# Scores, gate products and down projections issued in two halves around three products of the next weight unit

## The chip, the cores and the metric

The kernel runs on one core of one Trainium2 chip. The metric is the device time in microseconds (us); a run's time is that of its only core. Times of single executions come from the hardware profiler.

## What is computed

The reference is two transformer-like blocks on 256 tokens of width 1024, each with 16 meta tokens in front, all in float32. What matters here:

- Block one: a gated convolution mixer, then a layer of 16384 small experts. For each token and each of 8 heads a query of width 256 is scored against two sets of 128 sub-keys, `s1 = q[:128] @ keys1`, `s2 = q[128:] @ keys2`; the 16 best of each are paired, the 16 best pairs name experts, and a softmax gives their gates. The experts' output is `sum(gelu(u[e] . x) * gate[e] * v[e])`.
- Block two: two kinds of attention with gates, then a feed-forward part `(silu(h @ w_gate) * (h @ w_up)) @ w_down` with 2816 hidden columns.

The kernel does the expert layer densely: it computes `u . x` for all 16384 experts, multiplies by a gate that is zero nearly everywhere, and multiplies by `v`.

## The kernel before

**Units of weights.** All weights come as 453 units of 128 x 1024 floats. `load_to` (L124) starts the DMAs, five ahead. `split_to` (L145) splits each unit into a rounded half `hi` (ScalarE, L150) and the rest `lo` (VectorE, L152), two or three units ahead. `unit` (L155) hands out the next unit. A float32 product is then made of three rounded ones: hi x hi, hi x lo, lo x hi.

**Two ways to use a unit.** `mm_w` (L164) uses a unit as stationary weights: 8 slices of 128, three products each (L169 to L171), so 24 products with 256 moving columns into one PSUM bank. `mm_a` (L173) uses it as the moving side: two token halves, two column halves, three products each (L182 to L184), so 12 products with 512 columns into four banks that add up over many units.

**Plain float32 products.** Some small products are not split. They are single `matmul` calls with 128 columns on float32 data, and the trace has two records (passes) for each. The scores of a head (L539) are four such calls, so 8 passes; a gate group of four tokens (L675) is four calls, so 8 passes; there are 8 heads and 64 gate groups.

**The stages that the change touches.**

1. Route stage. The loop at L721 goes over 8 heads: two query units (`q`), then 7 expert units (`u`, `expert_in`, L694). After every unit `pull` (L709) lets VectorE's side work go on: a list `todo` of Python generators, each of which yields its estimated cost in us. `pull(us)` adds `us` to a credit, at most up to twice `us`, and runs the first generator of the list until the credit is spent; a `yield None` ends the pull at once. A head's `route` (L532) first yields None, then issues the scores on TensorE, copies them out (L540) and picks the best 16 (costs 9.3 in all). `decode` (L555) costs 19.1 and comes twice, after heads 3 and 7; `softmax` (L594) and `flip` (L609) follow the last route. A head's units bring 2 x 1.4 + 7 x 1.5 = 13.3 of credit.
2. Gate stage. When that list is empty, `gates` (L643) takes its place, 2.4 of credit for each `u` unit. Step g builds the two sides of group g on VectorE (`ga` L662, `gb` L666; before every eighth group also three one-hot instructions, L653 to L657), issues the four products of group g - 1 on TensorE (L675), and takes group g - 2 out of PSUM (L685, L687). So the passes of a group stand between two `u` units. What is left when the units run out is done in one go (L754), and only then do the `v` units begin.
3. Feed-forward. The loop at L1083 goes over 22 slices: `fg` and `fu` (24 products each, L1086, L1090), then the down projection `fd` of the slice two before (12 products, L1107). The last two `fd` units come together (L1109).

**What sets the order.** TensorE and the DMA queue of SyncE run in the order in which the Python program issues their instructions (`manual_schedule`, L272). VectorE and ScalarE are ordered by a scheduler. Every tile buffer is handed on by semaphores.

Of the kernel before, what the change touches and what calls it, by code (L numbers as in the profile page):

```python
# [1 line left out]

# [48 lines left out]
def two_blocks(ctx, tc, x, feats, vecs, w_in, w_out, w_q, keys, u, v, final_g, meta2, w_in2, lams, w_gate,  # L51
               w_br_sb, w_br_df, w_out2, w_fg, w_fu, w_fd, final_g2, gains, out):
    nc = tc.nc
# [107 lines left out]
        return ready[n]  # L161


    def mm_w(ps, a, cols):  # L164
        hi, lo = unit()
        ahi, alo = a
        for k in range(KC):
            ks = slice(k * P, (k + 1) * P)
            nc.tensor.matmul(ps, hi[:, ks], ahi[:, k, cols], start=(k == 0), stop=False)  # L169
            nc.tensor.matmul(ps, hi[:, ks], alo[:, k, cols], start=False, stop=False)  # L170
            nc.tensor.matmul(ps, lo[:, ks], ahi[:, k, cols], start=False, stop=(k == KC - 1))  # L171

    def mm_a(acc, parts, first, last):  # L173
        ws = [unit(1 if last else 2) for _ in parts]
        for t in range(2):
            ts = slice(t * P, (t + 1) * P)
            for n, ((ahi, alo), (hi, lo)) in enumerate(zip(parts, ws)):
                for b in range(2):
                    bs = slice(b * 512, (b + 1) * 512)
                    ps = acc[2 * t + b]  # L180
                    end = last and n == len(parts) - 1
                    nc.tensor.matmul(ps, ahi[:, ts], hi[:, bs], start=first and n == 0, stop=False)  # L182
                    nc.tensor.matmul(ps, ahi[:, ts], lo[:, bs], start=False, stop=False)  # L183
                    nc.tensor.matmul(ps, alo[:, ts], hi[:, bs], start=False, stop=end)  # L184

    def col(name, i):
        o = _OFF[name] + i
# [344 lines left out]
    def route(hd, qT, kt):  # L532
        yield None
        s = pr.tile([P, 2, 2, P], F32, tag="s", name=f"s{hd}", bufs=2)
        pss = mm_tile(f"sc{hd}")
        pv = pss.rearrange("p (t f n) -> p t f n", t=2, f=2)
        for t in range(2):
            for half in range(2):
                nc.tensor.matmul(pv[:, t, half, :], qT[half][:, t * P:(t + 1) * P], kt[:, half, :], start=True, stop=True)  # L539
        nc.scalar.activation(s, pv, AF.Copy)  # L540
        vv = pr.tile([P, 2, 2, TOPK], F32, tag="vv", name=f"vv{hd}", bufs=2)
        for t in range(2):
            for half in range(2):
                yield from top16(s[:, t, half, :], vv[:, t, half, :], iu_a[:, half, t, hd, :], 0.3)
        cand = pr.tile([P, 2, 88], F32, tag="cand", name=f"cand{hd}", bufs=2)
        nc.vector.tensor_tensor(cand[:, :, 0:16], vv[:, :, 0, 0:1].broadcast_to((P, 2, 16)), vv[:, :, 1, :], op=ALU.add)
        for a0, na, nb, o in ((1, 3, 8, 16), (4, 12, 4, 40)):
            nc.vector.tensor_tensor(cand[:, :, o:o + na * nb].rearrange("p t (a b) -> p t a b", a=na),
                                    vv[:, :, 0, a0:a0 + na].unsqueeze(3).broadcast_to((P, 2, na, nb)),
                                    vv[:, :, 1, :nb].unsqueeze(2).broadcast_to((P, 2, na, nb)), op=ALU.add)  # L550
        yield 0.7
        for t in range(2):
            yield from top16(cand[:, t, :], vals_a[:, t, hd, :], pos_a[:, t, hd, :], 0.26)
# [89 lines left out]
    def gates():  # L643
        pg, eT, gT, ah, al = (later[n] for n in ("pg", "eT", "gT", "ah", "al"))
        B32 = 32
        sides, banks = {}, {}
        for g in range(NG + 2):
            if g < NG:
                t0 = 4 * g
                if t0 % B32 == 0:  # L650
                    ts = slice(t0, t0 + B32)
                    o8 = pg.tile([P, B32, 8], F32, tag="o8", name=f"o8_{g}")
                    nc.vector.tensor_tensor(o8, ah[:, ts].unsqueeze(2).broadcast_to((P, B32, 8)),  # L653
                                            io128[:, :8].unsqueeze(1).broadcast_to((P, B32, 8)), op=ALU.is_equal)
                    nc.vector.tensor_tensor(o8, o8, gT[:, ts].unsqueeze(2).broadcast_to((P, B32, 8)), op=ALU.mult)
                    o16 = pg.tile([P, B32, TOPK], F32, tag="o16", name=f"o16_{g}")
                    nc.vector.tensor_tensor(o16, al[:, ts].unsqueeze(2).broadcast_to((P, B32, TOPK)),  # L657
                                            io16.unsqueeze(1).broadcast_to((P, B32, TOPK)), op=ALU.is_equal)
                    yield 1.6
                tl = slice(t0 % B32, t0 % B32 + 4)  # L660
                a = pg.tile([P, 4, P], F32, tag="ab", name=f"ga{g}", bufs=4)
                nc.vector.tensor_tensor(a.rearrange("p t (h l) -> p t h l", h=8),  # L662
                                        o8[:, tl, :].unsqueeze(3).broadcast_to((P, 4, 8, TOPK)),
                                        o16[:, tl, :].unsqueeze(2).broadcast_to((P, 4, 8, TOPK)), op=ALU.mult)
                b = pg.tile([P, 4, P], F32, tag="ab", name=f"gb{g}", bufs=4)
                nc.vector.tensor_tensor(b, eT[:, 1, t0:t0 + 4].unsqueeze(2).broadcast_to((P, 4, P)),  # L666
                                        io128.unsqueeze(1).broadcast_to((P, 4, P)), op=ALU.is_equal)
                sides[g] = (a, b)
                yield 1.4
            if 0 <= g - 1 < NG:  # L670
                a, b = sides.pop(g - 1)
                ps = at_tile(f"gp{g - 1}")
                p3 = ps.rearrange("p (c t) -> p c t", t=4)
                for i in range(4):
                    nc.tensor.matmul(p3[:, :, i], b[:, i, :], a[:, i, :], start=True, stop=True)  # L675
                banks[g - 1] = p3
            if g >= 2:
                j = g - 2
                p3 = banks.pop(j)
                n = seen[0]  # L680
                for tile_, c0, c1 in ((ew[0], 0, NA), (ew[1], NA, NK)):
                    m = min(max(n, c0), c1)
                    if m > c0:
                        o = tile_[:, j, :m - c0, :]
                        nc.vector.tensor_tensor(o, p3[:, c0:m, :], o, op=ALU.mult)  # L685
                    if m < c1:
                        nc.scalar.activation(tile_[:, j, m - c0:, :], p3[:, m:c1, :], AF.Copy)  # L687
                gated[0] = j + 1
                yield 0.2 + 0.55 * n / NK

    def chunk(c):
# [68 lines left out]
    def expert_w(i):  # L760
# [7 lines left out]
        wts[i] = hi2[:, 0, :], lo2[:, 0, :]  # L768
        wts[i + 1] = hi2[:, 1, :], lo2[:, 1, :]

    expert_w(0)
    while nu < NK:
        expert_in(nu)
# [309 lines left out]
    for m in range(NFF + 1):  # L1083
# [20 lines left out]
            nc.vector.tensor_tensor(lo, fa, hi.bitcast(F32), op=ALU.subtract)  # L1104
            prev.append((hi, lo))
        if 1 < m < NFF:
            mm_a(acc, [prev[m - 2]], m == 2, False)  # L1107
        elif m == NFF:
            mm_a(acc, prev[-2:], False, True)  # L1109
    table(AF.Sqrt)  # L1110
# [82 lines left out]
```

## Time and profile before

| what | value |
|---|---|
| median of 3 runs | 1479.19 us (1478.61 to 1486.41) |
| profiled execution, its own time | 1478.11 us |
| span of its instructions | 1476.4 us |
| mean granted TensorE clock | 0.997 |
| busy: TensorE products, weight loads, VectorE, ScalarE | 98%, 91%, 72%, 51% |
| route stage | about 125 to 377 us |
| gate stage with units, and its rest | 385 to 584 us, 584 to 597 us |
| feed-forward with down projections | about 1290 to 1469 us |

The span runs from the first to the last instruction; 1.7 us of the execution's own time lie around it. Starts of instructions are in us from the span's start, to 0.01 us. The end of a product is modelled, so the pace of TensorE is read from the starts: the start of one product to that of the next.

### The profile page before, as it was taken

How to read it: one execution, taken by the hardware profiler on the slowest of the kernel's cores; microseconds unless marked ns; L12 is line 12 of the kernel's file. 1: busy time of each engine (PE TensorE's matmuls, PEld its weight loads, DVE VectorE, ACT ScalarE, POOL GpSimd, SP SyncE). 2: the span in 40 equal slices, each digit the busy share in tenths (PEclk: the TensorE clock that was granted, in tenths of full speed). 3: DMA queues.
4: the chain of work that ended last, by engine and by line, in shares of the span. 5: the costliest groups of instructions: out<-in, count | busy, mean ns of one | idle time of the engine just before them, and what ended most of it. 6: DMA issues, size and time to landing. Idle time of an engine off the chain costs nothing.

```text
span 1476.4 us, 25739 instructions
## 1 busy us (share of the span) xinstructions
PE 1446.7 (98%) x10096; PEld 1338.5 (91%) x10096; DVE 1059.0 (72%) x1936; ACT 746.6 (51%) x1312; POOL 14.1 (1%) x32
## 2 busy tenths in 40 slices
PE   8999999999999999999999999999999999999998
PEld 7988999999999999788888888889998999899997
DVE  8987669779788999655555565755577776766665
ACT  7556444445444443344444445655455674554444
POOL 0010000000000000000000000100000000000000
PEclk9999999999999999999999999999999999999999
DMA  7626666665544444466666676633334456556662
GB/s 236 199 72 201 197 177 193 189 184 186 168 140 143 143 144 129 141 192 195 188 196 196 191 252 190 190 125 115 127 115 130 128 171 184 165 186 194 187 187 98
DMA packets 69816, 248.96 MB, mean 169 GB/s; under 512 B 7744, under 2 KB 9152, under 8 KB 69696
## 3 DMA queue, kind: packets, MB, share of 16 engines
q1 hardware_dynamic: 68544, 243.13, 52.9%
q0 software_dynamic: 1152, 4.19, 0.8%
q8 instruction: 79, 1.29, 0.4%
q14 instruction: 41, 0.34, 0.1%
HBM read 245.20 MB, written 2.10 MB: 168 GB/s over the span
## 4 chain that ended last, share of the span: by engine, by line
PE 93%; DVE 5%; issue 1%; DMA 0%; ACT 0%; SPq 0%; DVEq 0%; ACTq 0%
PE v L184 8%; PE v L182 8%; PE v L183 8%; PE u L171 7%; PE u L169 7%; PE u L170 7%; PE gp L675 4%; PE fg L170 1%; PE fu L171 1%; PE fg L171 1%; PE fu L170 1%; PE fd L184 1%; PE fu L169 1%; PE fg L169 1%; PE fd L183 1%; PE fd L182 1%
## 5 line engine op out<-in xcount | busy, mean ns | idle before, releaser
L152 DVE TENSOR_TENSOR lo<-raw,hi 128x1024 fp32r<-128x1024 f32 x453 | 552.9, 1223 | 241.4 <-ACT hi L150 239.9
L150 ACT ACTIVATE hi<-raw 128x1024 fp32r<-128x1024 f32 x453 | 478.6, 1058 | 469.7 <-PE u L170 122.7
L169 PE MATMUL u<-hThi,hi 128*128 128x256 f32 x1024 | 289.9, 283 | 0.0
L171 PE MATMUL u<-hThi,lo 128*128 128x256 f32 x1024 | 285.3, 279 | 0.1
L170 PE MATMUL u<-hTlo,hi 128*128 128x256 f32 x1024 | 284.9, 278 | 0.0
L182 PE MATMUL v<-hi,w_hi 128*128 128x512 f32 x512 | 199.3, 389 | 1.3 <-ACT w_hi L764 1.3
L184 PE MATMUL v<-hi,w_lo 128*128 128x512 f32 x512 | 199.3, 389 | 0.5 <-DVE w_lo L766 0.5
L183 PE MATMUL v<-lo,w_hi 128*128 128x512 f32 x512 | 199.2, 389 | 0.0
L170 PEld LDWEIGHTS u<-hTlo,hi 128*128 128x128 f32 x1024 | 194.0, 189 | 0.0
L171 PEld LDWEIGHTS u<-hThi,lo 128*128 128x128 f32 x1024 | 192.3, 188 | 0.8 <-DVE lo L152 0.7
L169 PEld LDWEIGHTS u<-hThi,hi 128*128 128x128 f32 x1024 | 192.5, 188 | 0.0
L182 PEld LDWEIGHTS v<-hi,w_hi 128*128 128x128 f32 x512 | 96.1, 188 | 21.4 <-ACT w_hi L764 1.5
L184 PEld LDWEIGHTS v<-hi,w_lo 128*128 128x128 f32 x512 | 96.1, 188 | 20.9 <-DVE w_lo L766 1.0
L183 PEld LDWEIGHTS v<-lo,w_hi 128*128 128x128 f32 x512 | 96.1, 188 | 20.1 <-DVE lo L152 0.2
L675 PE MATMUL gp<-ga,gb 128*128 128x128 f32 x512 | 66.6, 275 | 4.0 <-DVE gb L666 4.0
L764 ACT ACTIVATE w_hi<-ewa 128x512 fp32r<-128x512 f32 x48 | 30.2, 632 | 76.7 <-PE v L183 65.9
L675 PEld LDWEIGHTS gp<-ga,gb 128*128 128x128 f32 x512 | 61.7, 191 | 4.8 <-PE gp L675 3.6
L766 DVE TENSOR_TENSOR w_lo<-ewa,w_hi 128x512 fp32r<-128x512 f32 x48 | 33.2, 693 | 38.6 <-ACT w_hi L764 38.6
L662 DVE TENSOR_TENSOR ga<-o,o 128x512 f32<-128x512 f32 x64 | 44.0, 687 | 17.8 <-PE gp L675 17.3
L170 PE MATMUL fg<-hTlo,hi 128*128 128x256 f32 x176 | 49.2, 280 | 0.5 <-DVE hTlo L223 0.5
L169 PE MATMUL fg<-hThi,hi 128*128 128x256 f32 x176 | 49.3, 280 | 0.3 <-ACT hThi L222 0.3
L171 PE MATMUL fu<-hThi,lo 128*128 128x256 f32 x176 | 49.1, 279 | 0.0
(403 smaller groups left out, 2970.6 us busy)
## 6 DMA issues: line engine op xcount, KB each, us to landing
raw<-in_u_dram SPq DMA_DIRECT2D x128, 512.0 KB, 3.6
raw<-in_v_dram SPq DMA_DIRECT2D x128, 512.0 KB, 3.6
raw<-in_w_in_dram SPq DMA_DIRECT2D x67, 512.0 KB, 3.6
raw<-in_w_fg_dram SPq DMA_DIRECT2D x22, 512.0 KB, 3.6
raw<-in_w_fu_dram SPq DMA_DIRECT2D x22, 512.0 KB, 3.6
raw<-in_w_fd_dram SPq DMA_DIRECT2D x22, 512.0 KB, 3.6
raw<-in_w_out_dram SPq DMA_DIRECT2D x16, 512.0 KB, 3.6
raw<-in_w_q_dram SPq DMA_DIRECT2D x16, 512.0 KB, 4.3
```

The source lines that it names most:

```text
L150: latest["hi"] = nc.scalar.activation(hi, loaded[i], AF.Copy)
L152: latest["lo"] = nc.vector.tensor_tensor(lo, loaded[i], hi.bitcast(F32), op=ALU.subtract)
L169: nc.tensor.matmul(ps, hi[:, ks], ahi[:, k, cols], start=(k == 0), stop=False)
L170: nc.tensor.matmul(ps, hi[:, ks], alo[:, k, cols], start=False, stop=False)
L171: nc.tensor.matmul(ps, lo[:, ks], ahi[:, k, cols], start=False, stop=(k == KC - 1))
L182: nc.tensor.matmul(ps, ahi[:, ts], hi[:, bs], start=first and n == 0, stop=False)
L183: nc.tensor.matmul(ps, ahi[:, ts], lo[:, bs], start=False, stop=False)
L184: nc.tensor.matmul(ps, alo[:, ts], hi[:, bs], start=False, stop=end)
L662: nc.vector.tensor_tensor(a.rearrange("p t (h l) -> p t h l", h=8), o8[:, tl, :].unsqueeze(3).broadcast_to((P, 4, 8, TOPK)), o16[:, tl, :] ...
L675: nc.tensor.matmul(p3[:, :, i], b[:, i, :], a[:, i, :], start=True, stop=True)
L764: nc.scalar.activation(hi, a, AF.Copy)
L766: nc.vector.tensor_tensor(lo, a, hi.bitcast(F32), op=ALU.subtract)
```

## The change

Products can now be put off: `pend` is a list of pieces of work, and `flush(n)` issues the first n of them. `mm_w` issues the first half of what is pending before its first slice and the rest after the three products of its first slice. Scores, gate products and the down projections of the feed-forward part go through this list, each as two halves: two calls (4 passes) for scores and gates, one token half (6 products) for a down projection. `route` yields None a second time between the scores and their copy. `gates` and `mm_a` issue what is still pending before they go on. The down projections in the `v` stage, in the attention's output and the last two of the feed-forward part stay as they were.

```diff
+    pend = []
+
+    def flush(n=None):
+        for f in pend[:n]:
+            f()
+        del pend[:n]
+
     def mm_w(ps, a, cols):
         hi, lo = unit()
         ahi, alo = a
+        flush((len(pend) + 1) // 2)
         for k in range(KC):
+            if k == 1:
+                flush()
             ks = slice(k * P, (k + 1) * P)
...
-    def mm_a(acc, parts, first, last):
+    def mm_a(acc, parts, first, last, late=False):
         ws = [unit(1 if last else 2) for _ in parts]
-        for t in range(2):
+
+        def tokens(t):
             ts = slice(t * P, (t + 1) * P)
...
+        if late:
+            pend.extend(partial(tokens, t) for t in range(2))
+        else:
+            flush()
+            tokens(0)
+            tokens(1)
...
-        for t in range(2):
+
+        def scores(t):
             for half in range(2):
                 nc.tensor.matmul(pv[:, t, half, :], qT[half][:, t * P:(t + 1) * P], kt[:, half, :], start=True, stop=True)
+
+        pend.extend(partial(scores, t) for t in range(2))
+        yield None
+        flush()
         nc.scalar.activation(s, pv, AF.Copy)
...
         for g in range(NG + 2):
+            flush()
             if g < NG:
...
-                for i in range(4):
-                    nc.tensor.matmul(p3[:, :, i], b[:, i, :], a[:, i, :], start=True, stop=True)
+
+                def pair(i0, a=a, b=b, p3=p3):
+                    for i in (i0, i0 + 1):
+                        nc.tensor.matmul(p3[:, :, i], b[:, i, :], a[:, i, :], start=True, stop=True)
+
                 banks[g - 1] = p3
-            if g >= 2:
+                fresh = [partial(pair, 0), partial(pair, 2)]
+            else:
+                fresh = []
+            if g < 2:
+                pend.extend(fresh)
+            else:
...
                 gated[0] = j + 1
+                pend.extend(fresh)
                 yield 0.2 + 0.55 * n / NK
...
-            mm_a(acc, [prev[m - 2]], m == 2, False)
+            mm_a(acc, [prev[m - 2]], m == 2, False, late=True)
```

## Rows read from the trace of the kernel before

**Rows 1.** The page: busy times, and the chain that ended last, by engine.
```profile
PE 1446.7 (98%) x10096; PEld 1338.5 (91%) x10096; DVE 1059.0 (72%) x1936; ACT 746.6 (51%) x1312; POOL 14.1 (1%) x32
...
PE 93%; DVE 5%; issue 1%; DMA 0%; ACT 0%; SPq 0%; DVEq 0%; ACTq 0%
```

**Rows 2.** Windows: length, busy us (instructions) by engine, granted clock, DMA share, GB/s.
```profile
124.50:376.60 252.10, 251.89 (x2179) 250.93 (x2178) 197.14 (x558) 127.75 (x191) 0.00 (x0) 1.00 0.61 188
385.40:583.70 198.30, 198.30 (x1731) 198.30 (x1730) 180.56 (x330) 87.75 (x235) 0.00 (x0) 1.00 0.46 142
583.70:596.60 12.90, 7.61 (x58) 6.61 (x56) 12.80 (x29) 2.02 (x5) 0.00 (x0) 1.00 0.13 45
```

**Rows 3.** Timeline of TensorE, the scores of heads 0 to 7: start us, us, instruction.
```profile
135.72 1.05 PE L539 MATMUL sc<-kt,qT 128*128 128x128 f32 x8
...
162.06 1.06 PE L539 MATMUL sc<-kt,qT 128*128 128x128 f32 x8
...
187.45 1.05 PE L539 MATMUL sc<-kt,qT 128*128 128x128 f32 x8
...
213.78 1.06 PE L539 MATMUL sc<-kt,qT 128*128 128x128 f32 x8
...
267.28 1.05 PE L539 MATMUL sc<-kt,qT 128*128 128x128 f32 x8
...
285.13 1.06 PE L539 MATMUL sc<-kt,qT 128*128 128x128 f32 x8
...
302.37 1.05 PE L539 MATMUL sc<-kt,qT 128*128 128x128 f32 x8
...
323.05 1.06 PE L539 MATMUL sc<-kt,qT 128*128 128x128 f32 x8
```

**Rows 4.** Timeline of TensorE, three gate groups and second products behind two of them.
```profile
480.00 1.05 PE L675 MATMUL gp<-ga,gb 128*128 128x128 f32 x8
...
483.72 1.06 PE L675 MATMUL gp<-ga,gb 128*128 128x128 f32 x8
...
484.74 0.28 PE L170 MATMUL u<-hTlo,hi 128*128 128x256 f32 x1
...
487.36 1.05 PE L675 MATMUL gp<-ga,gb 128*128 128x128 f32 x8
...
488.37 0.28 PE L170 MATMUL u<-hTlo,hi 128*128 128x256 f32 x1
```

**Rows 5.** Timeline of TensorE, first product of down projections 0, 1 and 2.
```profile
1301.94 0.39 PE L182 MATMUL fd<-hi,f_hi 128*128 128x512 f32 x1
...
1310.20 0.39 PE L182 MATMUL fd<-hi,f_hi 128*128 128x512 f32 x1
...
1318.65 0.39 PE L182 MATMUL fd<-hi,f_hi 128*128 128x512 f32 x1
```

**Rows 6.** Timeline of TensorE, two gate groups of the rest.
```profile
588.61 1.13 PE L675 MATMUL gp<-ga,gb 128*128 128x128 f32 x8 [0.73 <-DVE gb L666]
590.48 1.13 PE L675 MATMUL gp<-ga,gb 128*128 128x128 f32 x8 [0.74 <-DVE gb L666]
```

**Rows 7.** Timeline of VectorE, start of a one-hot block, and what follows.
```profile
544.01 0.41 DVE L653 TENSOR_TENSOR o<-eT,io 128x256 f32<-128x256 f32 x1
544.34 0.68 DVE L657 TENSOR_TENSOR o<-al,io 128x512 f32<-128x512 f32 x1
544.94 1.22 DVE L152 TENSOR_TENSOR lo<-raw,hi 128x1024 fp32r<-128x1024 f32 x1
```

**Rows 8.** Timeline of TensorE, a group of four passes amid 256-column products.
```profile
1290.19 0.60 PE L231 MATMUL rsf_b<-rsf_d,ones 128*128 128x128 f32 x4
...
1290.75 0.28 PE L170 MATMUL fg<-hTlo,hi 128*128 128x256 f32 x1
```

**Rows 9.** Waits between 120 and 600 us: who for whom: us, times, longest us.
```profile
DVE ga L662 <- PE gp L675: 17.3, 32, 1.3
...
PEld u L171 <- DVE lo L152: 0.7, 3, 0.3
```

More of the change, by code (lines that the diff above doesn't have):

```diff
@@ L1 @@
 from contextlib import ExitStack
+from functools import partial
 import concourse.bass as bass
@@ L769, in expert_w @@
         wts[i + 1] = hi2[:, 1, :], lo2[:, 1, :]
+    assert not pend
     expert_w(0)
```

## Prediction, made before the changed kernel had run

> **What bounds the kernel now.** I read the page first: TensorE is busy for 98% of the span and makes 93% of the chain that ended last [rows 1], so only its pace and its holes count. The windows by stage come next: in the route stage and the gate stage TensorE has next to no hole, at full granted clock; VectorE is busy for 180.6 of 198.3 us (91%) in the gate stage. Between 583.7 and 596.6 us it is the other way round: VectorE is busy for 12.8 of 12.9 us and TensorE for 7.6 [rows 2]. That is the rest of the gate work, when no unit is left.
>
> The pace inside a full stage has to be read from starts, in the timeline. From one of the first four scores to the next lie 9 units, 216 products, each time the same work. They take 26.34 us, then 25.39, then 26.33 [rows 3]. The difference of 0.95 us is 4.4 ns a product. The reader is to see that it alternates with the scores: 8 passes go by and the pace is the other one. Six units from 267.28 us take 17.85, the next six 17.24 [rows 3]. The gate stage does the same per unit: 3.72 us from group to group, then 3.64 [rows 4]; and so does the feed-forward part per pair of units, 8.26 us between down projections, then 8.45 [rows 5]. The 95 products from 1290.75 to 1301.94 us take 117.8 ns each [rows 5, 8]: that is the slow pace, and the fast one is then 113.4. So TensorE keeps one of two paces for as long as 256-column products follow each other, and a whole group of scores, gates or a down projection turns the pace over.
>
> **What the change adds and removes.** No product, DMA or VectorE instruction comes or goes; what changes is the order on TensorE, and the planner's bookkeeping.
>
> *The halves.* I expect a half to turn the pace over as a whole does. From fast, the first half leaves slow; three products on, the second half enters slow and leaves fast. So the route stage, fast up to its first scores, stays fast. Slow now are the units behind the first, third, fifth and seventh scores, 9 + 9 + 6 + 7 = 31 [rows 3]. 24 products x 4.4 ns is 0.106 us a unit: **-3.3 us**. In the gate stage every second unit is slow, 26 to 27 of the 53 that will follow a group: **-2.8 us**.
>
> The feed-forward part begins slow [rows 8], so its first half group would leave fast. But three products are few, and I take the pace not to have settled by the second half, which then enters as if slow too and leaves fast. Then all gaps are 8.26 us, and 9 of the 19 are 8.45 now: 9 x 0.19 = **-1.7 us**. If slow were carried through instead, the 10 fast gaps would become slow: +1.9. No row shows an entry after three products; these are the ends, and I take the first because a settled slow entry left fast each time.
>
> *The price of splitting.* From the start of a gate group to the second product behind it 1.01 to 1.02 us go by [rows 4], for 8 passes and one product. For 4 passes the one row is at 1290 us: 0.56 [rows 8]. Two halves with three products are then 0.56 + 2 x 0.118 + 0.56 = 1.36 us up to the second product after; the whole group and three products more are 1.02 + 3 x 0.113 = 1.36. So it is free to the rounding of the rows, 0.01 a time; settling after each half may cost as much again. I take 0.02 for 53 gate groups and 8 scores, whose passes are alike, and 0.01 for 19 down projections: **+1.4 us**; the ends are 0 and twice that.
>
> *The second None.* This moves the plan, and it costs. The copy of the scores comes one unit later, and the pull is broken off there, so that credit above the cap is lost. In heads 0 to 3 that costs nothing later, because the queue runs dry before the next head anyway (9.3 of work against 13.3 of credit). From then on decode's 19.1 keep the queue full. I followed the credit unit by unit: before, the queue is empty after unit 73, and the units end with 7 gate groups to do, which is what the trace has (56 weight loads in the rest [rows 2]). After, it is empty after unit 77, and 11 groups remain. Each of the rest takes 1.87 us, since TensorE waits for `gb` [rows 6], against 0.9 in the stage (1.02 less one product of 0.12 [rows 4]). The one-hot block of group 56 falls into the rest as well: 0.33 + 0.60 us from start to start, and 0.33 for its third, which has the size of the first: 1.26 [rows 7]. 4 x 1.87 + 1.26 - 4 x 0.9 = **+5.1 us**. Bounds: 3.9 (the block hides) and 6.5 (one group more and some arrears).
>
> *Waits.* The second half of a gate group ends three products later, 0.35 us, and `ga` two groups on waits for it: VectorE waits there 32 times now, 17.3 us in all [rows 9]. Behind it on VectorE stand the `lo` of coming units and `gb`. It would wait 0.35 longer once and then run with that lag; the sides are needed a unit later (3.6 us [rows 4]), so this hides. Without that slack it would show as gaps before gate products, at most 0.35 us x 53. In the feed-forward part ScalarE's split into the buffer of the `fd` unit is let go 0.35 us later too, and is used two units on, over 5 us: 0. SyncE's DMAs are issued by `unit` in the same order as before, and none waits for another thing: 0. POOL's queue is not passed. TensorE's weight loads wait for `lo` 0.7 us in all [rows 9], in the route stage; with the side work moved that may go or double: -0.7 to +0.7.
>
> **The sum**: -3.3 - 2.8 - 1.7 + 1.4 + 5.1 = -1.3 us. Against the profiled execution's own 1478.1 that is 1476.8. The median of the three runs lies 1.1 higher; I put the forecast in between, at **1477.2 us**.
>
> **A rule that speaks against it.** The rows show two paces for one and the same product, 117.8 and 113.4 ns [rows 3, 5, 8]. The Trainium skill, page "TensorE: Matmul & The Clock Gate", section "Back-to-back issue gap", gives one gap per width at full clock, N/2.4 + 2.5 ns, so 109 ns for 256 columns, whatever came before; by it the order of issue would be worth nothing, and the sum would hold the price and the rest alone. The rows disagree with it: two paces, both longer than the rule's.
>
> **Rivals.**
> 1. *The down projections carry the slow pace.* As forecast, but +1.9 for -1.7: 1480.4. For it: the part begins slow [rows 8], and two turns bring back what was. Against it: only that three products are few. Chance 0.20.
> 2. *Two halves count as one group* and turn the pace over once, so it goes on alternating. Price and rest are left: 1478.1 + 1.4 + 5.1 = 1484.6. For it: three products are few. Against it: nothing but that each group turned it so far. The skill's one-gap rule comes out here as well. Chance 0.15.
> 3. *Slower: a half group always leaves TensorE slow.* It decides at the first scores, 135.72 us. For it: the one group of four passes amid such products comes from slow and is followed by slow [rows 8]. Against it: it has other operands, and whole groups from slow left fast. Now fast would become slow: in the route stage 53 units (2115 products besides the scores [rows 2] are 88 units, less 31 and the 4 before the first scores), in the gate stage 27, so 80 x 0.106 = 8.5, and 10 x 0.19 = 1.9 in the feed-forward part; with 1.4 and 5.1 that is +16.9: 1495.0. Chance 0.12.
> 4. *The rest does not grow*, because VectorE makes up for the later start: -3.3 - 2.8 - 1.7 + 1.4 = -6.4, 1471.7. Against it: 91% busy [rows 2]. Chance 0.05.
>
> The forecast has 0.45; 0.03 is for what I don't see.
>
> **The numbers.** 0.5% (7.4 us) is about what a measurement of this kernel can tell from no change. Forecast and rivals 1 and 2 lie within it, rival 3 above, rival 4 at its lower edge. Faster 0.05, same 0.81, slower 0.14. The range takes in rivals 1 and 2, and below the forecast the bounds of the price (-1.4), of the rest (-1.2) and of the waits (-0.7): 1473.0 to 1486.0.
>
> **What would show it.** Right: scores with nine units between them near 25.4 us apart every time; gate groups 3.64 us apart every time; 88 passes in the rest, which lasts 21.6 us where it lasted 12.9; down projections 8.26 us apart throughout. Wrong: distances that still alternate (rival 2) or all have the upper value (rival 3), 8.45 us between down projections (rival 1), 56 passes in the rest (rival 4).

## The result and the profile after

The changed kernel's median is 1491.47 us (8 runs, 1481.71 to 1497.02) against 1480.12 for the kernel before (8 runs, 1478.61 to 1486.41): the ratio is 1.0064, with a 95% interval of 1.0046 to 1.0082. Timed again later it was 1488.57 (12 runs, 1481.29 to 1493.20), ratio 1.0051 (1.0034 to 1.0068). The forecast was 1477.2, the range 1473.0 to 1486.0: too low, and the sign is the wrong one. The 20 times also lie far apart: 8 between 1481.3 and 1485.8, 12 between 1487.9 and 1497.0.

The profiled execution took 1484.49 us (span 1482.8), 6.4 more than that of before. Its page, busy times and chain, answers to [rows 1]:

```profile
PE 1450.1 (98%) x10096; PEld 1342.4 (91%) x10096; DVE 1059.7 (71%) x1936; ACT 746.6 (50%) x1300; POOL 14.1 (1%) x32
...
PE 95%; DVE 3%; DMA 1%; issue 0%; ACT 0%; SPq 0%; POOL 0%; DVEq 0%; ACTq 0%
```

No work came or went, TensorE is as full as before, so the time is in its pace and in the order. First the scores, in the timeline of TensorE (start, length, instruction; first halves of heads 0 to 3):

```profile
136.20 0.60 PE L560 MATMUL sc<-kt,qT 128*128 128x128 f32 x4
...
161.61 0.60 PE L560 MATMUL sc<-kt,qT 128*128 128x128 f32 x4
...
187.01 0.60 PE L560 MATMUL sc<-kt,qT 128*128 128x128 f32 x4
...
212.42 0.60 PE L560 MATMUL sc<-kt,qT 128*128 128x128 f32 x4
```

They are 25.41, 25.40 and 25.41 us apart, where before 26.34 and 25.39 took turns [rows 3]. The reader sees the mechanism of the forecast at work: two halves give the pace back. But the stage did not stay fast. Further on in the same timeline, products of one unit:

```profile
232.50 0.28 PE L182 MATMUL u<-hTlo,hi 128*128 128x256 f32 x1
232.61 0.38 PE L183 MATMUL u<-hThi,lo 128*128 128x256 f32 x1
232.82 0.29 PE L181 MATMUL u<-hThi,hi 128*128 128x256 f32 x1
...
234.60 0.28 PE L181 MATMUL u<-hThi,hi 128*128 128x256 f32 x1
...
235.66 0.28 PE L181 MATMUL u<-hThi,hi 128*128 128x256 f32 x1
```

and in the timeline of VectorE what the product of 232.61 needs, its `lo`:

```profile
230.19 1.22 DVE L614 TENSOR_TENSOR oh<-oh,ifl 128x1024 f32<-128x1024 f32 x1
231.32 1.22 DVE L153 TENSOR_TENSOR lo<-raw,hi 128x1024 fp32r<-128x1024 f32 x1
```

The `lo` stood behind a multiply of `decode` and ends at 232.54. The product that reads it takes 0.21 us to the next start, 0.10 more than its neighbours. Before it the pace is 113.3 ns; from 234.60 to 235.66 lie 9 products, 117.8 ns each. This slow pace goes through the last four scores unchanged to the end of the stage (a second gap, of 163 ns at 252.50 us, left it slow): 1293 slow products, 879 fast ones (counted by the distance of starts; before 807 and 1270).

The gate stage, gate groups in the timeline of TensorE:

```profile
405.91 0.60 PE L703 MATMUL gp<-ga,gb 128*128 128x128 f32 x4
406.71 0.60 PE L703 MATMUL gp<-ga,gb 128*128 128x128 f32 x4
409.62 1.06 PE L703 MATMUL gp<-ga,gb 128*128 128x128 f32 x8
413.26 1.05 PE L703 MATMUL gp<-ga,gb 128*128 128x128 f32 x8
416.98 1.06 PE L703 MATMUL gp<-ga,gb 128*128 128x128 f32 x8
```

One group is split, the next three are whole, and the distances still go 3.64, 3.72. In the whole stage the trace has 29 lines of 8 passes, 7 of 12 and 27 of 4, so 17 groups are split and 36 not. 636 of 1081 products are slow (622 of 1196 before). Gate stage and rest in the windows (columns as in [rows 2]):

```profile
397.57:581.45 183.88, 183.88 (x1602) 183.88 (x1601) 167.30 (x307) 81.15 (x215) 0.00 (x0) 1.00 0.45 142
581.45:603.22 21.77, 13.50 (x92) 12.09 (x90) 21.42 (x48) 2.08 (x5) 0.00 (x0) 0.92 0.08 25
```

The rest lasts 21.77 us (12.9 to 13.1 before [rows 2]) and holds 88 passes (56 before). VectorE's wait for a gate bank in the list of waits is no longer than before [rows 9]:

```profile
DVE ga L688 <- PE gp L703: 15.3, 29, 1.3
```

The down projections, first products in the timeline of TensorE, answer to [rows 5]:

```profile
1309.88 0.39 PE L195 MATMUL fd<-hi,f_hi 128*128 128x512 f32 x1
...
1318.15 0.39 PE L195 MATMUL fd<-hi,f_hi 128*128 128x512 f32 x1
...
1326.41 0.39 PE L195 MATMUL fd<-hi,f_hi 128*128 128x512 f32 x1
```

8.27 and 8.26 us apart: fast throughout, in this execution.

### The profile page after: what moved, and what is told of

It reads as the page before. It is cut to its first block, busy times and chain, and to the rows that moved or that the text cites. A ratio compares the mean times of both kernels' runs of the same rounds, so it can differ in the third digit from the quotient of the medians.

```text
span 1482.8 us, 25725 instructions
## 1 busy us (share of the span) xinstructions
PE 1450.1 (98%) x10096; PEld 1342.4 (91%) x10096; DVE 1059.7 (71%) x1936; ACT 746.6 (50%) x1300; POOL 14.1 (1%) x32
## 4 chain that ended last, share of the span: by engine, by line
PE 95%; DVE 3%; DMA 1%; issue 0%; ACT 0%; SPq 0%; POOL 0%; DVEq 0%; ACTq 0%
PE u L181 8%; PE u L183 8%; PE u L182 8%; PE v L196 7%; PE v L197 7%; PE v L195 7%; PE gp L703 3%; PE fg L182 1%; PE fd L197 1%; PE fd L196 1%; PE fg L183 1%; PE fd L195 1%; PE fg L181 1%; PE fu L183 1%; PE fu L182 1%; PE fu L181 1%
## 5 line engine op out<-in xcount | busy, mean ns | idle before, releaser
L195 PEld LDWEIGHTS v<-hi,w_hi 128*128 128x128 f32 x512 | 96.1, 188 | 21.6 <-ACT w_hi L799 1.5
L703 PE MATMUL gp<-ga,gb 128*128 128x128 f32 x512 | 70.9, 280 | 7.0 <-DVE gb L692 7.0
L183 PE MATMUL fg<-hThi,lo 128*128 128x256 f32 x176 | 48.8, 277 | 0.0
```

## The experiments

Two questions were open: what the parts of the change cost one by one, and why the times lie so far apart. The table gives the profiled execution of each kernel, in us: its own time, the route stage from the first `q` product to the first transpose of `flip`, its slow products, the gate stage, the rest, and the feed-forward part from the first product of the first down projection to the last product of the nineteenth.

| kernel | time | route | slow in it | gate | rest | feed-forward |
|---|---|---|---|---|---|---|
| before | 1478.11 | 252.1 | 807 | 198.1 | 13.05 | 152.92 |
| changed | 1484.49 | 263.7 | 1293 | 183.9 | 21.78 | 151.71 |
| e1 one None | 1476.41 | 250.6 | 130 | 198.2 | 13.05 | 151.71 |
| e2 None only | 1483.65 | 264.1 | 1439 | 183.5 | 21.78 | 152.92 |
| e3 down only | 1480.60 | 253.2 | 922 | 198.1 | 13.05 | 151.71 |
| e4 scores only | 1476.82 | 250.6 | 86 | 198.1 | 13.05 | 152.92 |
| e5 gates split | 1477.34 | 249.0 | 205 | 196.6 | 13.05 | 155.08 |
| e6 transposes | 1479.99 | 250.3 | 206 | 200.6 | 13.06 | 151.71 |
| e10 first scores whole | 1486.25 | 255.9 | 2014 | 198.2 | 13.05 | 155.08 |
| repeat 1 (changed) | 1482.35 | 259.8 | 94 | 183.9 | 21.77 | 155.08 |
| repeat 2 (changed) | 1484.13 | 263.7 | 1178 | 183.9 | 22.03 | 151.71 |
| again (changed) | 1485.22 | 259.9 | 209 | 183.9 | 21.78 | 155.08 |
| e11 light decode | 1481.50 | 259.0 | 37 | 183.9 | 21.77 | 151.71 |
| repeat 3 (changed) | 1482.74 | 259.9 | 94 | 183.9 | 21.78 | 155.08 |
| repeat 4 (changed) | 1486.10 | 261.4 | 92 | 183.9 | 21.78 | 155.08 |
| repeat 5 (changed) | 1485.55 | 260.9 | 41 | 183.5 | 22.03 | 151.71 |
| e12 first whole, two None | 1490.67 | 268.2 | 2066 | 183.9 | 22.03 | 151.71 |
| repeat 6 (changed) | 1490.00 | 269.0 | 2141 | 183.9 | 22.03 | 151.71 |

With the second None the route holds four units more, 96 products or 10.9 us at the fast pace, so 252.1 before stands against 263.0 there. In the kernels with halves for the down projections the last column holds three products of the next unit more, 0.34 us at the fast pace. From the first product of the first down projection to the start of the last product of the last one, the same work in every kernel, it is 166.78 us before, and 165.23 (fast) or 168.78 (slow) in the changed kernel.

**e1: the change with one None, so with the plan of before.**

```diff
     def route(hd, qT, kt):
-        yield None
```

> The changed kernel with the first None of route taken out, so that a route has one None as before. Theory A (two halves give the pace back, so TensorE keeps whatever pace the last disturbance left, for hundreds of us; the plan's later start costs 5.1 us by itself): the rest of the gate work is back at 7 groups and about 12.9 us, the time is some 5 us below the changed kernel's, and single runs still scatter over 5 to 12 us, since a wait in the route stage still decides the pace of all that follows. Theory B (only the plan costs): the time is that of the kernel before within 1 us, and runs scatter no more than its own do, about 3 us.

Measured: 1477.93 us (10 runs), 0.9986 of before (0.9972 to 1.0). The halves by themselves cost nothing; the median is 2.5 us lower, and the interval reaches from no gain to 4.1 us.

**e2: the second None alone, everything else as before.**

```diff
+        yield None
         nc.scalar.activation(s, pv, AF.Copy)
```

> The kernel before with a second None between the scores and their copy, all groups issued whole. Theories A and B both: 11 groups in the rest, 21.6 us, +5.1 us (1483 to 1485). Theory A besides: distances between scores still alternate between the two paces, and the runs scatter as little as those of the kernel before. If instead the time stays within 1.5 us of before, the longer rest is paid back elsewhere and the plan is not a cost.

Measured: 1485.90 us (6 runs, 1483.65 to 1488.69), 1.0047 (1.0032 to 1.0061), +5.4 against the 1480.46 of before. The rest has its 88 passes and 21.78 us here too. The plan alone makes the kernel slower, by about what the forecast gave it.

**e3: halves for the down projections alone.** `late=True` in the feed-forward part; scores and gates as before.

> The kernel before with the down projections of the feed-forward part alone in two halves. Theory A: within a run all 19 distances between first products of down projections are equal, 8.26 us if the part begins fast and 8.45 us if it begins slow; time -1.7 or +1.9 us against before, and which one can differ from run to run. Theory C (a second half three products on always leaves fast, as forecast): all at 8.26 us whatever the part begins with, -1.7 us.

Measured: 1480.45 us (10 runs), 1.0006 (0.9992 to 1.002). The profiled part is 1.2 us shorter in the table's window, 1.55 over the same work; the whole kernel is not measurably faster.

**e4: halves for the scores alone**, with one None.

> The kernel before with the scores alone in two halves, one None. Theory A: from the first to the fourth scores nine units take 25.4 us each time; behind that the pace is the one that the waits for lo left (between about 225 and 255 us), and it stays until the transposes of flip near 377 us, also across the scores of heads 4 to 7; time between -3.3 us (all fast) and +4 us (slow from 235 us on). Forecast as it stood: all distances fast, -3.3 us.

Measured: 1477.92 us (10 runs), 0.9987 (0.9972 to 1.0003). The window of its route stage, the stretch at its start, and the list of waits in the stage:

```profile
124.90:375.50 250.60, 250.39 (x2179) 249.51 (x2178) 196.98 (x557) 128.65 (x191) 0.00 (x0) 0.99 0.61 189
...
121.90:128.70 6.80, 5.75 (x27) 5.27 (x27) 5.31 (x8) 3.77 (x6) 0.00 (x0) 0.50 0.09 34
```

```profile
PEld u L183 <- DVE lo L153: 1.0, 4, 0.3
```

Here the scores did what the forecast wanted: 86 slow products for 807. By 4.4 ns each that is 3.2 us; the stage is 1.5 shorter. The difference is not in the waits: 1.0 us of waits for `lo` stand here, and as many before, 0.7 for `u` [rows 9] and in the same list

```profile
PEld q L171 <- DVE lo L152: 0.3, 1, 0.3
```

It is in the second window: this route starts at half clock. Its first scores come 10.04 us after its first product; in e5 and e10, with the same products ahead of them and full clock, it is 8.47 us. Without these 1.6 us the stage would be 3.1 us shorter than before. e5, which starts at full clock, has that directly (249.0); e1 starts at half clock as e4 does.

**Repeats 1 and 2: the changed kernel, unedited.** Repeats 1 to 6 are single profiled executions of it.

> The changed kernel once more, unedited, for a second profile. Theory A (the pace is carried): same order of instructions, but another pace can be held in the route stage behind the waits for lo, and in the feed-forward part from its first units on; whatever the time differs from 1484.5 us is found as 4.4 ns a product (slow less fast) in these two stages, up to 4 us in the feed-forward part. Theory B (something else scatters): the paces are as in the first profile and the difference lies elsewhere.

> The same as the look before, a third profile of the changed kernel: Theory A: times of 1490 us and more show the slow pace in both stages, times near 1482 the fast pace in at least one. Theory B: no such relation.

Repeat 1 has a fast route and a slow feed-forward part, repeat 2 the reverse. Of repeat 1 the route's window, its waits for `lo`, and its down projections:

```profile
124.80:384.60 259.80, 259.59 (x2275) 258.67 (x2273) 201.77 (x562) 133.94 (x199) 0.00 (x0) 1.00 0.61 190
```

```profile
PEld u L183 <- DVE lo L153: 0.7, 3, 0.3
```

```profile
1304.19 0.39 PE L195 MATMUL fd<-hi,f_hi 128*128 128x512 f32 x1
...
1312.64 0.39 PE L195 MATMUL fd<-hi,f_hi 128*128 128x512 f32 x1
...
1321.09 0.39 PE L195 MATMUL fd<-hi,f_hi 128*128 128x512 f32 x1
```

8.45 us apart, both times, where the execution above has 8.27. The same instructions, the other pace, and it is kept throughout (155.08 us for 151.71).

**e5: gate groups split where a unit follows**, on e1.

```diff
         for g in range(NG + 2):
-            flush()
...
             else:
+                flush()
                 j = g - 2
```

> As e1_one_none, but pending gate products are issued only before the eviction that needs them, so that by the planner 49 groups of the stage go out in halves and 8 whole (in the changed kernel 13 and 40). Theory A: the pace turns 8 times in the gate stage instead of at most groups, in long stretches; the slow share then depends on where they lie, between 20% and 60% of the products, and the time is within 1.5 us of e1_one_none. Forecast's view (split groups stay fast): slow share under 20%, 2 us below e1_one_none.

Measured: 1479.40 us (10 runs), 0.9983 (0.9964 to 1.0002). Now the trace has 93 lines of 4 passes and 7 of 12, so 50 groups of 57 are split, 193 of 1121 products are slow, and the gate stage is 1.5 us shorter. 429 fewer slow products are worth 1.9; the 0.4 between is the price of 50 splits, under 0.01 us each. In the whole kernel no gain is clear of noise.

**e7 and e8: how many parts, and how far apart**, both on e3. e7 issues a down projection in three parts of four products; e8 puts one product between the halves.

```diff
-        flush((len(pend) + 1) // 2)
...
-            if k == 1:
-                flush()
+            if k < 3:
+                flush(1)
...
+            pend.extend(partial(some, calls[i:i + 4]) for i in (0, 4, 8))
```

> The kernel before with the down projections alone in three parts of four products, three products of the next unit between part and part. Theory A (each part turns the pace once, so an odd number of parts turns it over): the distances between first products of down projections alternate as in the kernel before, one fast and one slow by about 0.2 us, 1 us slower or faster at most. Theory C (any split leaves fast): all distances equal.

```diff
-            if k == 1:
-                flush()
             ks = slice(k * P, (k + 1) * P)
             nc.tensor.matmul(ps, hi[:, ks], ahi[:, k, cols], start=(k == 0), stop=False)
+            flush()
```

> The kernel before with the down projections alone in two halves, with one product of the next unit between them in place of three. Theory A: two turns as with three products, so all distances equal (8.26 or 8.45 us). Theory D (one product is too few for the pace to turn, two halves count as one group): the distances alternate.

One execution each, 1479.91 and 1484.47 us. In e7 the down projections start at 1303.31, 1311.76, 1320.04 and 1328.49, so 8.45, 8.28, 8.45 apart. In the timeline of e8:

```profile
1308.15 0.39 PE L194 MATMUL fd<-hi,f_hi 128*128 128x512 f32 x1
...
1316.59 0.39 PE L194 MATMUL fd<-hi,f_hi 128*128 128x512 f32 x1
...
1324.86 0.39 PE L194 MATMUL fd<-hi,f_hi 128*128 128x512 f32 x1
...
1333.29 0.39 PE L194 MATMUL fd<-hi,f_hi 128*128 128x512 f32 x1
```

8.44, 8.27, 8.43. Three parts turn the pace an odd number of times, and it alternates. Two halves with one product between count as one group, in this one execution. So rival 2's mechanism exists, but not at three products.

**Again: the changed kernel, timed a second time** (12 runs, in the first paragraph).

> The changed kernel unedited, timed again beside the others of this group on one chip. Theory A: its runs spread over about 1481 to 1497 us, since the route stage (up to 9 us between all fast and all slow) and the feed-forward part (3.4 us) each keep the pace that a wait left; the profile's time follows from these two paces. Theory B: a constant surplus.

**e6: six transposes ahead of the feed-forward part**, on e5, to start it at the fast pace as `flip` seems to start the gate stage.

```diff
         across(pb, cols, rsf, "rsf")
+        spare = mm_tile("spare")
+        for j in range(6):
+            nc.tensor.transpose(spare[:, j % 4 * P:(j % 4 + 1) * P], ident, ident)
```

> e5_gates_split with six transposes behind the first pair of feed-forward units (0.66 us), since the six transposes of flip were followed by the fast pace in every profile, from either pace. Theory A with that: the feed-forward distances are 8.26 us in every profile, the time is 1 to 2 us below e5_gates_split in the median, about 1476, which is below the kernel before. If transposes don't set the pace, the feed-forward part can still be at 8.43 us, and the time is e5's plus 0.7.

Measured: 1478.65 us (11 runs), 0.9988 (0.9975 to 1.0002). The part was fast in this profile, but it is fast in eight of the fourteen others with halves there too. In the same execution the gate stage was slow for 1090 of 1121 products, right after `flip`'s own six transposes, and repeat 5 also leaves `flip` at the slow pace. They are no sure reset. Inconclusive.

**e10: one turn too few**, e1 with head 0's scores whole.

```diff
         pend.extend(partial(scores, t) for t in range(2))
+        if hd == 0:
+            flush()
```

> e1_one_none with the scores of the first head alone issued whole, so that the pace is turned once at about 135 us and given back at each later head. Theory A: the route stage is slow from 136 us until a wait for lo changes it, 9 units 26.3 us apart where they were 25.4, at least 3 units groups of nine (2.9 us) and up to 8.5 us more than e1_one_none; so one turn of the pace alone explains times like the slow ones of the changed kernel. Theory B: the time of e1_one_none.

Measured: 1483.55 us (10 runs, 1474.95 to 1486.52), 1.0008 (0.999 to 1.0026). Scores in the timeline of TensorE:

```profile
133.87 1.05 PE L559 MATMUL sc<-kt,qT 128*128 128x128 f32 x8
...
160.20 0.61 PE L559 MATMUL sc<-kt,qT 128*128 128x128 f32 x4
...
186.54 0.60 PE L559 MATMUL sc<-kt,qT 128*128 128x128 f32 x4
```

26.33 and 26.34 us apart, and 2014 of 2082 products slow: a single turn at 134 us is carried for 247 us, to the end of the stage. That costs 5.3 us of route over e1 (255.9 against 250.6), not 1884 x 4.4 ns = 8.3. Of the 3.0 between, 1.6 is e1's start at half clock, which e10 does not have: from the first scores to `flip` it is 247.4 us against 240.5. The rest is gaps at late `lo`, 1.4 us of them in e1 by the distance of starts: the list of waits of this stage has none for `lo` any more. At the slow pace VectorE is in time. Four of the ten times are below 1480 us; no profile shows what their routes did.

**e11: the changed kernel with less for VectorE to do in decode.** It leaves out 14 of the 16 columns of the multiply by the first indices.

```diff
-                nc.vector.tensor_tensor(o4, o4, if_a[:, half, t, hs, :].unsqueeze(2).broadcast_to((P, 4, TOPK, TOPK)), op=ALU.mult)
+                o1 = o4[:, :, :2, :]
+                nc.vector.tensor_tensor(o1, o1, if_a[:, half, t, hs, :].unsqueeze(2).broadcast_to((P, 4, 2, TOPK)), op=ALU.mult)
```

> The changed kernel with its plan untouched, but in decode the multiply of the one-hot block with the first indices covers 2 of 16 columns, so most of that multiply is left out (8 instructions of about 1.2 us become 8 of about 0.3). VectorE is then less late with lo during decode. Theory (a wait for lo turns TensorE's pace, halves never turn it back): the gaps of 197 to 213 ns at 230 to 233 us vanish, the fast pace lasts through the route stage, under 300 of its 2170 products are slow, and the timed median falls from 1488.6 to 1491.5 to between 1482 and 1486, although no product goes. Rival (the slow stretches have another source, and VectorE's lateness only coincides): slow stretches of more than 300 products in the route stage as in the changed kernel, and a median of 1488 or more.

Measured: 1484.57 us (8 runs, 1481.50 to 1493.96), 1.0045 (1.0023 to 1.0067). The median fell into the range that the theory gave and the route was fast but for 37 products. The gaps at `lo` that were left turned nothing for long. But 3 of the 8 times are still over 1491 us, where the changed kernel has 12 of 20 over 1487: so few runs can't tell the two shares apart. That a late `lo` of decode can start a slow stretch is seen in the profiles; that fewer of them lower the time is not shown by this run.

**Repeats 3 to 5: the changed kernel, for an execution over 1488 us.**

> The changed kernel once more, for an execution above 1488 us, which no profile has shown yet. Theory: its route stage is slow for over 1200 products, its feed-forward part slow throughout, and its v stage over 352 us; each product of the route that is slow costs 4.4 ns. Rival: such a time has another place, a hole or a clock drop.

> As the look before. Theory: route slow products x 4.4 ns, plus 3.4 us if the feed-forward part is slow, plus what the v stage is longer than 349.1 us, plus 1479.0 give the execution's time within 1.5 us. Rival: they do not.

> As the look before. Theory: route slow products x 4.4 ns, plus 3.4 us if the feed-forward part is slow, plus what the v stage is longer than 349.1 us, plus 1479.0 give the execution's time within 1.5 us. Rival: they do not.

None was over 1488. The sum gives 1482.8 for repeat 3 (measured 1482.74), 1484.8 for repeat 4 (1486.10) and 1483.3 for repeat 5 (1485.55), which misses by 2.3. Repeats 4 and 5 have in common what the theory did not hold, a route stage that starts at half clock. Of repeat 4 (window columns as in [rows 2]):

```profile
121.80:128.60 6.80, 5.75 (x27) 5.28 (x27) 5.31 (x8) 3.76 (x6) 0.00 (x0) 0.50 0.09 33
```

**e12 and repeat 6: a slow route under the new plan.** e12 is the changed kernel with e10's edit; repeat 6 is the changed kernel.

> The changed kernel, but the scores of head 0 whole, one turn instead of two. Theory (executions of the changed kernel above 1488 us are those whose route stage is slow throughout, by a wait or by a slow start): the profile shows over 1900 slow products in the route stage and its own time is 1490 to 1494 us, in the upper cluster of the changed kernel's times; those executions that start the route slow become fast, so that times near 1482 also occur, and the clusters change places. Rival (the upper cluster has a source outside the route): a profile with a slow route lies below 1488, or times above 1497 appear, because the slow route comes on top of that source.

> The changed kernel once more. Theory: route slow products x 4.4 ns, plus 3.4 us if the feed-forward part is slow, plus what the v stage is longer than 349.1 us, plus 1479.0 give the execution's time within 1.5 us. Rival: they do not.

e12: 1488.80 us (6 runs, 1487.03 to 1491.83), 1.0062 (1.005 to 1.0074); its profile at 1490.67 has 2066 slow products in the route, as the theory had it. No time near 1482 came, so that half of the expectation failed. Repeat 6 is the execution that was wanted, 1490.00 us. Its windows, and its scores in the timeline of TensorE:

```profile
122.00:128.80 6.80, 5.75 (x27) 5.25 (x26) 5.30 (x8) 3.79 (x6) 0.00 (x0) 0.50 0.11 42
128.80:394.00 265.20, 265.20 (x2256) 265.20 (x2256) 199.76 (x559) 131.64 (x196) 0.00 (x0) 1.00 0.61 187
```

```profile
138.13 0.61 PE L560 MATMUL sc<-kt,qT 128*128 128x128 f32 x4
...
164.47 0.61 PE L560 MATMUL sc<-kt,qT 128*128 128x128 f32 x4
...
190.80 0.60 PE L560 MATMUL sc<-kt,qT 128*128 128x128 f32 x4
```

It starts at half clock (1.2 GHz), comes out of it at the slow pace, and the halves keep that pace: 26.34 and 26.33 us between scores, 2141 slow products, TensorE without a hole from 128.8 to 394.0 us. The unedited kernel does by itself what e12 makes it do. The route takes 9.2 us longer than in repeat 1, of which about 1.6 is the start at half clock. The sum of the earlier expectation gives 1490.5.

## Why the prediction was wrong

**What held.** Each half turns the pace, two with three products between give it back, three parts do not: scores and down projections show it, and e7 and e8 bound it. The price of splitting was right or high (e5). The second None costs what the forecast said: "followed the credit unit by unit" gave 11 groups, 88 passes and 21.6 us, the trace has 88 and 21.77; e2 measures +5.4 for +5.1. With that alone the kernel is slower than before. The gains that should pay for it are what failed.

**"So the route stage, fast up to its first scores, stays fast": -3.3.** This is the step that failed most. The pace is turned by more than the groups. The forecast followed groups and took the stage's first pace as given. The trace of before already had a turn with no group near it, in the timeline of TensorE:

```profile
242.24 0.35 PE L171 MATMUL u<-hThi,lo 128*128 128x256 f32 x1
242.43 0.28 PE L169 MATMUL u<-hThi,hi 128*128 128x256 f32 x1
...
242.90 0.28 PE L170 MATMUL u<-hTlo,hi 128*128 128x256 f32 x1
```

Up to the first of these the pace is 113.3 ns, behind the second it is 117.5, for 47 products; at 248.0 us another gap turns it back. In the 8 profiles of the unedited changed kernel the route stays fast in five (in one of them, again, but for 20 us), is turned slow for good by a late `lo` of head 3's decode in two (the profile above and repeat 2), and starts slow in one (repeat 6). With whole groups the next one turns such a slip over, so that slow and fast stretches take turns whatever happens (807 of 2077 products slow before, 1439 of 2187 in e2). With halves the groups turn nothing back; only another late `lo` did, in the profile of the second timing ("again"). There the pace was turned slow at 232.1 us, and in the timeline of TensorE

```profile
251.41 0.28 PE L181 MATMUL u<-hThi,hi 128*128 128x256 f32 x1
...
252.00 0.33 PE L183 MATMUL q<-hThi,lo 128*128 128x256 f32 x1
...
259.78 0.28 PE L182 MATMUL u<-hTlo,hi 128*128 128x256 f32 x1
...
260.57 0.28 PE L183 MATMUL u<-hThi,lo 128*128 128x256 f32 x1
```

five products take 0.59 us up to a gap of 171 ns at 252.00, and further on seven take 0.79 us: 118 ns each, then 113. Where the route was fast, the size of the term was right: 3.1 us in e4 and e5 (e4 without its half-clock start). Against the 263.0 that the old route would last with four units more, the term was -3.2 in repeat 1, +0.7 in the profile above, +6.0 in repeat 6, of which 1.6 is the start at half clock.

**"TensorE's weight loads wait for `lo` 0.7 us in all [rows 9], in the route stage; with the side work moved that may go or double: -0.7 to +0.7."** It was 1.0 in all, with the row for `q`, and the waits were priced by their own length. Behind one of 0.10 us at 232.6 us over a thousand products were slow.

**"In the gate stage every second unit is slow, 26 to 27 of the 53": -2.8.** It was no gain at all: 183.9 us against 183.5 in e2, with the same plan and whole groups. The new `flush()` at the top of the loop of `gates` issues whatever is pending, and most pulls go through it: 36 of the 53 groups came whole. That could be read in the diff. With 50 of 57 split (e5) it was -1.5.

**"Three products are few": -1.7.** They are enough; one product is few (e8). So the part carries the pace it starts with: fast in four of the eight profiles, slow in the other four. Over the same work that is -1.55 or +2.0 us (165.23 or 168.78 for 166.78), near the sizes of the forecast and of rival 1, but four times each, where the forecast gave 0.45 to 0.20. Its reason, that the second half leaves fast whatever the part begins with, is refuted.

**The profiled sum.** Plan +5.1 and route +0.7 make +5.8; gate stage +0.4 (183.9 against e2's 183.5), a later start +0.5, `v` stage +0.4, a half-clock stretch in the products behind it +1.5, feed-forward part and the units ahead of it -1.55 and -0.6 bring it to 6.45, where the two profiles differ by 6.4. For repeat 6 the route is +6.0, the `v` stage +1.9, the rest 0.25 longer and the half-clock stretch behind `v` not there, and the sum comes to 11.95 for 11.9 measured. So the times of the changed kernel are a mixture, and the range ended at 1486.0, below its upper part. (Its lower end, 1473.0, is not what its bounds add up to either: 1477.2 less 1.4, 1.2 and 0.7 is 1473.9.) Rival 3 had a size near these times, but its reason, that a half always leaves slow, is refuted by the scores above.

**What makes the `v` stage last 349.1 to 353.8 us.** The traces show two things. Of the profile of again, two rows of the list of waits and a window:

```profile
DVE gain L830 <- DMA gain<-in_gains_dram: 4.9, 1, 4.9
...
PEld v L196 <- DVE lo L153: 3.2, 1, 3.2
```

```profile
864.20:867.60 3.40, 3.40 (x9) 2.68 (x10) 2.68 (x3) 0.00 (x0) 0.00 (x0) 0.52 0.70 216
```

VectorE waits for the DMA of another operand, `gain`, and the `lo` behind it comes late to TensorE: 3.2 us here, 0.5 to 2.6 in five other profiles of the changed kernel, where `gain` waits 2.1 to 4.3 us, and nothing in repeats 1 and 3, where it waits 1.7 and 1.5. And in five of the eight a stretch at half clock, like that of the last row, falls into the stage: about 1.7 us.

**What stays open.** 12 of the 20 times are over 1487 us, but only one of the eight profiles is. That its slow start is what all twelve have was argued from repeat 6 and e12, not shown, and two things on record stand against taking it for granted. The three profiles of the changed kernel that start the route at half clock (repeats 4 to 6) have a mean granted clock of 0.993, the other five 0.995 or 0.996; five of the twelve have 0.995. And a route turned slow by a late `lo` can reach such times as well: the sum of the earlier expectation, with 1293 slow products and a slow feed-forward part, gives an estimate of 1488.1 to 1492.8, by the `v` stage. No profile shows that combination.

Nine of the profiles in the table and of e7 and e8 start the route at half clock: e1, e3, e4, e6, e8, repeats 4 to 6 and e12. Eight come out of it fast, repeat 6 alone slow. e2 starts slow at full clock, all 91 products that were counted ahead of its first scores. What decides the pace at the start of a stage, or after a late operand, I can't say, nor what the two paces are inside TensorE.

## What to carry to other kernels

Before an order is arranged so that a state of the machine is kept, ask what sets that state and what will correct it if it is set wrong: an order that alternates gets the mean, one that preserves gets whatever the first disturbance left. Where a change works through a queue of pending work, count in the new code how often the queue is emptied at a place other than the one that was meant. A change of the plan that costs 5 us is worth timing by itself: without the second None the halves are no slower than the kernel before (e1, 0.9986).

## What the runs showed that was not expected

- The pace has a memory as long as the stage: 113.3 or 117.7 ns for the same product, for up to 2141 products on end and across scores, at a granted clock of 1.00. The Trainium skill, page "TensorE: Matmul & The Clock Gate", section "Back-to-back issue gap", gives N/2.4 + 2.5 ns at full clock, 109 ns for 256 columns; it calls that the gap of an isolated product, and its figures for a stream with weight loads are for 128 and 512 columns alone. The prediction held it against a stream. The runs show two gaps there, both longer than 109 ns.
- A gap of 197 to 215 ns at a late `lo`, between 229 and 238 us, came in 15 of the profiles, always from the fast pace. In nine the pace went on fast, in six (gaps of 213, 200, 212, 197, 197 and 215 ns) it was slow for the next 165 to 167 products. The length of the gap does not tell which.
- A route that is slow from its first scores on has no gap at a `lo` at all (repeat 6, e10 and e12): TensorE reaches each `lo` later, and nothing comes that could turn it back. A route that turned slow between 229 and 238 us still had one, of 163 to 174 ns at 250 to 257 us, in all six profiles; in four it turned fast there (e3, e5, e6, again), in two it stayed slow (the profile above, e8).
- A start at half clock, 6.8 us at 0.50, costs about 1.6 us by itself: repeat 6's first scores come 13.1 us after the first product, 11.2 in the profile above, and 0.3 of that is the slow pace of 78 products.
